# A decoder layer on one NeuronCore: 14 of 16 gate tiles by seven block products in a pass of their own, and the heads' filling laid out anew

## The chip, the core and the metric

The kernel is one program on one of the eight cores of a Trainium2 chip. The metric is the device time of one execution in microseconds (us). Five engines work at the same time, each through its own queue in its own order: PE (TensorE, matrix products and transposes into PSUM banks), DVE (VectorE), ACT (ScalarE), POOL (GpSimd) and SP (which here issues the DMAs). They wait for each other by semaphores.

## What is computed

A decoder layer on x (1024 tokens by 1024 channels, float32), cut here to what matters:

```python
x = x + 0.5 * swiglu(rms_norm(x, ffn1_norm), ...)          # 1024 -> 2816 -> 1024
h = rms_norm(x, mix_norm)
fq, fk, fv, f_logit, sq, sk, sv, g_fox, g_sb = split_columns(h @ w_in)
y_fox = forgetting_attention(rms_norm(fq), rms_norm(fk), fv, log_sigmoid(f_logit + bias))  # 8 heads of 64
y_sb  = stick_breaking_attention(sq, sk, sv)                                                # 8 heads of 64
merged = sigmoid(g_fox) * (y_fox @ w_branch_fox) + sigmoid(g_sb) * (y_sb @ w_branch_sb)
x = x + merged @ w_out
x = x + 0.5 * swiglu(rms_norm(x, ffn2_norm), ...)
x = x + sigmoid(rms_norm(x, ple_norm) @ w_ple_gate) * (p @ w_ple_proj)
```

The gates g_fox and g_sb are 2048 columns of h @ w_in, here 16 tiles of 128 channels by 1024 tokens. Forgetting attention is a causal softmax with a decay per key; stick-breaking attention weighs key s by a sigmoid times the product of (1 - sigmoid) over the keys between s and the query, a running product from right to left.

## The kernel before, in words

**Precision.** Every float32 operand of a product is split into a rounded high part (ACT copies) and a low part (the difference, by DVE or, for weights, by POOL: `wlow`, line 139). A product is three products: high·high, high·low, low·high. One gate tile is two halves of 512 tokens; one half is 3 x 8 matmuls of 128x512 (`feat_steps`, line 708).

**Seven block products.** The two feed-forward blocks don't multiply by the plain rule. `ffn` (line 380) cuts each pair of tiles into blocks and forms 7 products of 3 x 4 matmuls for what takes 8 by the plain rule (Winograd's form of Strassen's scheme; line 473 of the gate and up products, line 368 of the down product). The sums of blocks of h that it needs are made by the `combo_` functions: `a` turns a 128-token slice of the normalised h by transposes (line 228), the others make the sums and split them. The first block pair is partly taken by `plain` (line 428), plain products that run while the sums are made.

**The order.** Inside the feed-forward blocks all engines' orders are as written in the source. In attention, `pe(...)` ties PE's instructions to the written order, and `order("dve", ...)` and `order("act", ...)` tie some of those of DVE and ACT; the rest is placed by a scheduler when the program is built, and each engine then runs its list in order. A tile of a tag (`BUFS`, line 31) has a fixed number of buffers, and an instruction that writes one waits for the readers of what lay in it.

**Between the first feed-forward block and attention** (`mix_start`, line 1050). The last down products overlap with the norm of x; then come the value products of four heads (`v_units`, 8 units of one 128-token block each) and the query and key products of the first pair of forgetting heads (`fox_qk_units`, 8 units), each unit 24 matmuls of 256 or 264 columns (line 700). After unit 3 and unit 7 of a pair, the half of four units is normalised: ACT squares and copies (764, 765), DVE sums (766, 769), POOL takes the power -1/2 (770) and multiplies (772). Then come the sums of the forget gates (`forget_logs`, `forget_sums`, lines 909 and 910) and, plain, gate tiles 0 and 1 and the PLE projection (`p_units`, line 863).

**Stacks.** Per head, `fox_stack_units` turns the normalised queries and keys of one half of the tokens with four transposes (line 802, from the tile that line 772 wrote) and splits them into the tiles Q, KH and KL (787 to 790, two DMAs between partitions); `sb_stack_units` does so from products with 24 matmuls of 128x512 per half.

**The heads.** `attention` (line 1079) runs 16 heads, 8 forgetting (h 0 to 7) and 8 stick-breaking (h 8 to 15), each in four steps c = 0 to 3 of two 128-query blocks. A step does `scores` of its two blocks (PE lines 944 and 945) and then `apply` of the step before it: for each pair of key blocks, from the last to the first, four transposes of the weights (996), a high copy by ACT (998), a low part by DVE (999), and four value products (1018) that read both. In the stick-breaking heads ACT takes two sigmoids of the scores (952, 953), DVE does the running products (`scan`, 920) and POOL multiplies (967, 971). The scans of a step's first block are issued in `scores`; those of the second block (`later`) are issued inside `apply`, one after each low part.

**Filling.** `take` puts other matmuls between: 22 times per head (7, 4, 5 and 6 times in steps 0 to 3) it takes the next 1/22 of that head's entry of `fill`, a list of units written out by hand: value units, query and key units, the next head's stacks, and the plain gate tiles (`g_units`, line 821), tiles 2 to 15 in heads 2 to 15.

**After the heads** come the branch products, in which `gated` (line 1229) loads a gate half, takes its sigmoid (gates of the forgetting branch) and multiplies; the output product; and the second feed-forward block, entered through `second_entry` (line 1389), whose norm, transposes and sums run between the last output products and the first gate products.

Of the kernel before, what the change touches and what calls it, by code (L numbers as in the profile page):

```python
# [31 lines left out]
        "Q": 2, "KH": 2, "KL": 2, "Y": 2, "PT": 3}  # L32
# [4 lines left out]
def tile_hybrid_decoder_layer(  # L37
# [223 lines left out]
    def halves(N):  # L261
        return [(n["hi"], n["lo"]) for n in N]
# [117 lines left out]
    def ffn(N, wg, wu, wd, next_gain, resid, hid, tags, entry, tail):  # L380

        wsrc = [kp(w[0]) for w in (wg, wu)]
        wdown = wd[0].rearrange("(j k p) n -> k p j n", k=2, p=P)
        LA = 4
        nm_ = 2 * NF  # L390
# [4 lines left out]
        seqn += [(n, 1), (n - 1, 4), (n, 2), (n, 6), (n, 5), (n, 7), (n - 1, 3), (n, 3), (n, 4)]  # L395
# [9 lines left out]
        def load(n):  # L405
            f0 = n // 2 * 256
            W[n] = {"r": [slot(t, [P, 4, 256]) for t in tags["raw"].get(n, (("WH", "WH"), ("KH", "KL"))[n % 2])]}
            for kh in range(2):
                nc.sync.dma_start(W[n]["r"][kh][:], wsrc[n % 2][:, 4 * kh:4 * kh + 4, f0:f0 + 256])
# [23 lines left out]
        def silu(f_, half):  # L433
            if 0 not in E:
                E[0] = [slot(t, [P, 2, 512]) for t in ("GF", "RN")]
            nc.scalar.activation(E[0][f_][:, half, :], bank_of.pop("plain")[:], AF.Silu)
# [11 lines left out]
        def prep(n, m):  # L448
# [9 lines left out]
            if m == 3 and n + 2 < nm_:  # L458
                load(n + 2)
# [19 lines left out]

        def right(t, b, k):  # L480
            if isinstance(t, list):
                return t[2 * b + k // 2][:, k % 2, :]
            return t[:, b, k, :]

        def evict(n, m, ps):
# [8 lines left out]
            elif m == 7:  # L494
                nc.scalar.copy(e2[:, 1, :], ps[:])
                nc.vector.tensor_add(e2[:, 1, :], e2[:, 1, :], bank_of[n, "d"][:])
# [27 lines left out]
        C = {"w": {}, "t1": {}}  # L524

        def combo_a(q):

            h = N[1]["h"][q]
            cs = slice(q * P, (q + 1) * P)
            if q == 0:  # L530
                B[1], B[2] = N[0]["B"]
                B[3] = [slot("T", [P, 2, 512], F32R) for _ in range(4)]
                B["12"] = slot("X", [P, 2, 4, 512], F32R)
            w = C["w"][q] = slot(tags["w"][q], [P, 2, 4, P])
            v12, v22 = (turn(h, b, bank(cyc("t", ("pf", "av", "pf", "sc", "pt", "av", "pt", "sc")))) for b in range(2))
            nc.scalar.copy(w[:, 0], v12)
            nc.scalar.copy(w[:, 1], v22)
            split(B["12"][:, 0, :, cs], B["12"][:, 1, :, cs], w[:, 0], nc.scalar, nc.vector)
            for i in range(2):
                split(B[3][i][:, :, cs], B[3][2 + i][:, :, cs], w[:, 1, 2 * i:2 * i + 2], nc.scalar, nc.vector)  # L540

        def combo_t(q):

            cs = slice(q * P, (q + 1) * P)
            if q == 0:
                B[5] = slot("H", [P, 2, 4, 512], F32R)
            if q % 2 == 0:
                C["t1"][q // 2] = slot(("RN", "GF")[q // 2], [P, 2, 4, P])
            w, t1 = C["w"][q], C["t1"][q // 2][:, q % 2]
            nc.vector.tensor_sub(t1, w[:, 0], f(B[1][:, 0, :, cs]))  # L550
            nc.vector.tensor_sub(t1, t1, f(B[1][:, 1, :, cs]))
            nc.scalar.copy(B[5][:, 0, :, cs], t1)

        def combo_l(q):

            cs = slice(q * P, (q + 1) * P)
            nc.vector.tensor_sub(B[5][:, 1, :, cs], C["t1"][q // 2][:, q % 2], f(B[5][:, 0, :, cs]))

        def combo_u(q):

            w, t1 = C["w"][q], C["t1"][q // 2][:, q % 2]
            nc.vector.tensor_sub(w[:, 0], w[:, 1], w[:, 0])
            nc.vector.tensor_sub(w[:, 1], w[:, 1], t1)

        def combo_s(q, m):

            cs = slice(q * P, (q + 1) * P)
            if q == 0:
                B[m] = slot("H" if m == 6 else "X", [P, 2, 4, 512], F32R)
            split(B[m][:, 0, :, cs], B[m][:, 1, :, cs], C["w"][q][:, 7 - m], nc.scalar, nc.vector)  # L570

        def combo_d(q):

            cs = slice(q * P, (q + 1) * P)
            w = C["w"][q]
            nc.vector.tensor_sub(w[:, 0], f(B[2][:, 0, :, cs]), w[:, 1])
            nc.vector.tensor_add(w[:, 0], w[:, 0], f(B[2][:, 1, :, cs]))

        def combo_e(q):
            cs = slice(q * P, (q + 1) * P)  # L580
            if q == 0:
                B[4] = slot("X", [P, 2, 4, 512], F32R)
            split(B[4][:, 0, :, cs], B[4][:, 1, :, cs], C["w"][q][:, 0], nc.scalar, nc.vector)

        down = make_down(wdown, hid, [(0, 4), (4, 7), (7, 11)], 0.5, ("Y", "PT"))
        nxt = []

        def last_norms(i, t):
            if i == 4:
                norm_stat(nxt[0], t, ("PT", "PT", "KH", "KL")[t])  # L590
            elif i == 5:
                norm_mul(nxt[0], t)
            elif i == 6:
                if t == 3:
                    norm_post(nxt[0], 2, ps1)
                norm_stat(nxt[1], t, ("GF", "RN", "KH", "KL")[t])
                if t:
                    if t < 3:
                        norm_mul(nxt[1], t - 1)
                    norm_post(nxt[0], (None, 0, 1, 3)[t], ps1)  # L600
                for call in tail.get((i, t), ()):
                    call(nxt)

        manual[0] = True
        with tc.manual_schedule():
            entry(dict(a=combo_a, t=combo_t, l=combo_l, u=combo_u, s=combo_s, load=load, prep=prep, sums=sums, last_sum=last_sum, plain=plain, silu=silu, product=product, evict=evict))
            for s, (n, m) in enumerate(seqn):
                evict(n, m, product(n, m))
                if s == 0:
                    sums(2, nc.vector)  # L610
                    for q in range(4):
                        combo_s(q, 7)
                elif s == 2:
                    last_sum(1, nc.vector)
                    last_sum(2, nc.vector)
                if 1 < s < 6:
                    combo_d(s - 2)
                if 2 < s < 7:
                    combo_e(s - 3)
                if s + LA < len(seqn):  # L620
                    prep(*seqn[s + LA])
# [22 lines left out]
            for s, (c, i) in enumerate(steps):  # L644
# [18 lines left out]
                if final:  # L663
                    if i == 3:
                        nxt.append(norm_begin(X[0], next_gain))
                        nxt.append(norm_begin(X[1], next_gain, nxt[0]))
                    for call in tail.get(i, ()):
                        call(X)
                for t in range(4):
                    matmuls(t)  # L670
                    evict_down(t)
                    if final:
                        last_norms(i, t)
            norm_mul(nxt[1], 2)
            norm_mul(nxt[1], 3)
            tail["end"](X, nxt)
        manual[0] = False
        return X, nxt
# [621 lines left out]
    def products(F, rest=()):  # L1300

        F["load"](2)
        for i in range(2):
            F["plain"](1, 0, (i,))
            for q in rest[i:i + 1]:
                F["a"](q)
# [242 lines left out]
```

## Time and profile before

| | |
|---|---|
| median of 3 runs | 2273.2 us (2272.91 to 2273.32) |
| the profiled execution's own time | 2274.11 us |
| its span, first to last instruction | 2272.4 us |
| PE busy | 2248.2 us of the span (99%) |
| DVE, ACT, POOL busy | 1462.3, 977.4, 828.8 us |
| first forgetting head starts | 755.7 us from the span's start |
| first stick-breaking head starts | 1049.7 us |
| last value product of the last head | 1393.3 us |

Times in the views count from the span's start. A view of groups gives the line, engine and operation, what is written from what, the shape, the count, then the busy time and the mean duration of one (ns), then the idle time of the engine before them and what ended it. A timeline row is start, duration, engine, line, operation, and in brackets the engine's idle time before it. A matmul row is longer than the distance to the next matmul, since matmuls are pipelined; what a matmul costs is the distance between starts.

### The profile page before, as it was taken

What the parts mean: (1) busy time and instruction counts of PE and PEld (TensorE: products, weight loads), DVE (VectorE), ACT (ScalarE), POOL (GpSimd) and SP (SyncE); (2) the same over time, 40 slices, a digit from 0 to 9 for tenths busy, and PEclk for the clock granted to TensorE, in tenths of its full rate; (3) what the DMA queues carried; (4) which work ended last, traced back from release to release, by engine and by line L of the source; (5) the groups of instructions that cost most, each with busy time, mean ns of one, the idle gap of its engine ahead of it and who ended that gap; (6) DMA issues with size and microseconds to landing.
All of it is one profiled execution on the core that took longest, in us unless ns stands there. A gap on an engine that the chain in (4) does not pass through costs nothing. (4 is left out here: it accounts for less than half of the span.)

```text
span 2272.4 us, 30639 instructions
## 1 busy us (share of the span) xinstructions
PE 2248.2 (99%) x11462; PEld 1911.9 (84%) x11462; DVE 1462.3 (64%) x2199; ACT 977.4 (43%) x1741; POOL 828.8 (36%) x762
## 2 busy tenths in 40 slices
PE   8999999999999999999999999999999999999999
PEld 6888888888899999988988888888888888888888
DVE  8845555688863466666667676889655555778753
ACT  6333333333353555555555564246333333434431
POOL 2344444300033456554645644410544444200121
PEclk9999999999999999999999999999999999999999
DMA  4232323484333322132224245822423232756132
GB/s 139 99 120 85 124 84 125 152 302 171 103 122 121 103 80 75 48 89 70 52 56 116 61 144 176 299 109 65 139 84 125 84 125 80 263 194 218 60 103 84
DMA packets 187655, 275.49 MB, mean 121 GB/s; under 512 B 27113, under 2 KB 109417, under 8 KB 187506
## 3 DMA queue, kind: packets, MB, share of 16 engines
q1 hardware_dynamic: 187504, 273.53, 35.9%
q8 instruction: 90, 1.47, 0.3%
q14 instruction: 59, 0.48, 0.1%
q10 hardware_dynamic: 2, 0.00, 0.0%
HBM read 189.83 MB, written 75.27 MB: 117 GB/s over the span
## 5 line engine op out<-in xcount | busy, mean ns | idle before, releaser
L368 PE MATMUL ps<-H,H 128*128 128x512 f32 x2184 | 497.7, 389 | 1.2 <-DVE X L376 1.2
L368 PEld LDWEIGHTS ps<-H,H 128*128 128x128 f32 x2184 | 409.4, 188 | 86.7 <-issue 2.0
L473 PE MATMUL ps<-H,WL 128*128 128x512 f32 x1008 | 239.3, 389 | 0.8 <-ACT WL L105 0.8
L473 PEld LDWEIGHTS ps<-H,WL 128*128 128x128 f32 x1008 | 189.1, 188 | 40.4 <-ACT WL L105 1.2
L708 PE MATMUL ps<-H,WH 128*128 128x512 f32 x768 | 210.3, 401 | 1.1 <-DVE PT L831 1.1
L708 PEld LDWEIGHTS ps<-H,WH 128*128 128x128 f32 x768 | 136.4, 188 | 24.1 <-DVE PT L831 1.5
L139 POOL TENSOR_TENSOR WL<-RAW,WH 128x512 fp32r<-128x512 f32 (+1 forms) x108 | 127.4, 1200 | 77.5 <-ACT WH L129 71.9
L139 POOL TENSOR_TENSOR WL<-Y,WH 128x512 fp32r<-128x512 f32 (+1 forms) x10 | 14.4, 1466 | 382.6 <-ACT WH L129 382.6
L999 DVE TENSOR_TENSOR PT<-ps,PT 128x512 fp32r<-128x512 f32 (+1 forms) x160 | 101.1, 633 | 76.1 <-ACT PT L998 75.1
L473 PE MATMUL ps<-H,Q 128*128 128x512 f32 x600 | 143.1, 389 | 0.0
L376 DVE SCALAR_TENSOR_TENSOR X<-ps,X 128x512 f32<-128x512 f32 x168 | 109.0, 685 | 50.9 <-PE ps L368 50.9
L700 PE MATMUL ps<-WH,H 128*128 128x256 f32 (+1 forms) x896 | 132.0, 287 | 1.9 <-DVE X L106 1.0
L473 PEld LDWEIGHTS ps<-H,Q 128*128 128x128 f32 x600 | 112.6, 188 | 23.4
L998 ACT CAST PT<-ps 128x512 fp32r<-128x512 f32 (+1 forms) x160 | 87.3, 548 | 95.8 <-PE ps L996 92.3
L473 PE MATMUL ps<-X,WL 128*128 128x512 f32 x504 | 121.1, 389 | 0.0
L700 PEld LDWEIGHTS ps<-WH,H 128*128 128x128 f32 x896 | 116.9, 190 | 3.7 <-DVE X L106 1.4
L1018 PE MATMUL ps<-PT,X 128*128 128x256 f32 (+1 forms) x640 | 106.2, 283 | 6.1 <-DVE PT L999 6.0
L473 PEld LDWEIGHTS ps<-X,WL 128*128 128x128 f32 x504 | 94.6, 188 | 19.6
L1018 PEld LDWEIGHTS ps<-PT,X 128*128 128x128 f32 x640 | 94.5, 190 | 19.1 <-DVE PT L999 9.7
L708 PE MATMUL ps<-H,WL 128*128 128x512 f32 x384 | 108.3, 398 | 0.0
L957 POOL TENSOR_TENSOR T<-T,l 128x128 f32<-128x128 f32 (+3 forms) x64 | 73.3, 1150 | 88.5 <-DVE l L956 86.1
L269 POOL TENSOR_TENSOR PT<-GF,RN 128x512 f32<-128x512 f32 x20 | 33.1, 1655 | 186.0 <-DVE GF L516 101.8
(400 smaller groups left out, 4735.3 us busy)
## 6 DMA issues: line engine op xcount, KB each, us to landing
hidden<-PT SPq DMA_DIRECT2D x40, 512.0 KB, 3.1
WH<-in_ffn_w_gate_dram SPq DMA_DIRECT2D x38, 512.0 KB, 5.3
Q<-hidden SPq DMA_DIRECT2D x24, 512.0 KB, 6.1
hidden<-RN SPq DMA_DIRECT2D x22, 512.0 KB, 2.7
RAW<-in_w_in_dram SPq DMA_DIRECT2D x22, 512.0 KB, 4.3
KH<-in_ffn_w_up_dram SPq DMA_DIRECT2D x20, 512.0 KB, 6.2
KL<-in_ffn_w_up_dram SPq DMA_DIRECT2D x20, 512.0 KB, 6.8
T<-in_ffn_w_down_dram SPq DMA_DIRECT2D x20, 512.0 KB, 4.3
```

Source lines behind the costliest of these rows:

```text
L139: ins = eng_lo.tensor_sub(lo[part], raw[part], f(hi[part]))
L269: eng.tensor_add(s12[:, 0, :], g1[:, 1, :], g2[:, 1, :])
L368: pe(nc.tensor.matmul(groups[g][t][:], act[:, a, k, t * P:(t + 1) * P], wt[:, b, k, :], start=(fresh and n == 0), stop=(i in (6, 1, 4) and ...
L376: nc.vector.scalar_tensor_tensor(xs, groups[g][t][:], scale, xs, ALU.mult, ALU.add)
L473: pe(nc.tensor.matmul(ps[:], hl[:, a, k, :], rhs(m, b, k), start=(first and i == 0), stop=(final and i == 11), skip_group_check=True))
L700: pe(nc.tensor.matmul(ps[:, :n], hT[t // 4][a][:, k, (t % 4) * P:(t % 4 + 1) * P], w[k // 4][b][:, k % 4, :n], start=(i == 0), stop=(i == ...
L708: pe(nc.tensor.matmul(ps[:], w[a][:, k, :], hT[half][b][:, k, :], start=(i == 0), stop=(i == 23)))
L957: nc.gpsimd.tensor_mul(T[:, :n], T[:, :n], l[:].broadcast_to([P, n]))
L998: high = nc.scalar.copy(pt[:, 0, :width], ps[:, :width])
L999: low = nc.vector.tensor_sub(pt[:, 1, :width], ps[:, :width], f(pt[:, 0, :width]))
L1018: pe(nc.tensor.matmul(o, lh, r, start=(kpair == c and i == 0), stop=(kpair == 0 and i == 3)))
```

## The change

`ffn`'s block products become `make_up`, used by both feed-forward blocks and by a new pass over the gates; `up_begin`, `up_step` and `up_first` are what `second_entry` did, and are now called by the gates' pass as well. The main parts:

```diff
-        "Q": 2, "KH": 2, "KL": 2, "Y": 2, "PT": 3}
+        "Q": 2, "KH": 2, "KL": 2, "Y": 2, "PT": 3, "Z": 2}
...
+    NG = 7
     def mix_start():
...
+        def gate_out(n, i, e):
+            nc.sync.dma_start(gd[2 * n + i].rearrange("p (h n) -> p h n", h=2), e[:])
...
+        F = make_up(N, lambda n: kp(win)[:, :, GFOX + n * 256:GFOX + n * 256 + 256], NG, tags_g, AF.Sigmoid, gate_out, load_qk)
...
-        def end(X, N):
-            hT.extend(halves(N))
-            store_x(X, 1)
...
-            side = posts(N[1], (24, 64, 104, 144), lambda: bank("pt"))
-            side[48] = [lambda: mx["qk"].update(w=[wsplit(raws["qk"][kh], 4, 256, tags[kh]) for kh in range(2)])]
-            weave(seq(*[g for _, g in mx["u1"][:4] + mx["u2"][:4]]), side)
+        def end():
+            up_first(N, F)
+            seqn = up_order(NG)
+            L = len(seqn)
+            for s, (n, m) in enumerate(seqn):
+                evict(n, m, F.product(n, m))
+                F.begin(s)
+                if s + 4 < L:
+                    F.prep(*seqn[s + 4])
...
+            for _, g in mx["u1"]:
+                run(g)
```

In attention, the part ahead of the heads and the filling:

```diff
-        run_all(u1[4:])
         sums = forget_logs(wk)
-        run_all(p0[:1] + u2[4:])
+        run_all(p0[:1] + u2)
         forget_sums(sums)
         f0 = fst(0, any_bank)
-        run_all(g0[:1] + f0[:1] + p0[1:3] + g0[1:] + f0[1:] + p0[3:] + g1[:1] + p1 + g1[1:])
+        run_all(f0[:1] + p0[1:3] + f0[1:] + p0[3:] + p1)
-        fill.append(mix(fst(1), fox_qk_units(fox_pairs[1], qk[1])))
-        fill.append(uv[:4] + mix(fst(2), uv[4:]))
-        fill.append(mix(fst(3), g + uq[:4]))
-        fill.append(uq[4:] + mix(fst(4), g_units(3)))
-        fill.append(mix(fst(5), fox_qk_units(fox_pairs[3], qk[3])))
-        fill.append(uv[:4] + mix(u, uv[4:]))
...
-        fill.append(u + g9[1:] + g10)
-        u, g11, g12 = sst(13), g_units(11), g_units(12)
-        fill.append(u + g11 + g12[:1])
...
+        fill = [mix(fst(1), qk1[:6]),
+                qk1[6:] + fst(2) + vx[:4],
+                fst(3) + vx[4:] + uq2[:2],
+                uq2[2:] + fst(4),
+                fst(5) + uq3[:5],
+                uq3[5:] + fst(6) + vy[:2],
+                fst(7) + vy[2:7],
+                vy[7:] + s8,
+                s9 + vz[:2],
+                vz[2:6] + s10,
+                vz[6:] + s11,
+                s12 + g14[:1],
+                g14[1:] + s13,
+                s14 + g15[:1],
+                g15[1:] + s15,
+                fox_branch[:7]]
```

Here `fst(h)` are the two stack units of forgetting head h, `sst(h)` or `s8` to `s15` those of stick-breaking heads, `qk1`, `uq2`, `uq3` (`uq`) the query and key units of the second to fourth pair, `uv`, `vx`, `vy`, `vz` value units, `g14` a gate tile's two halves. All gates are now written out after their sigmoid, and `gated` loses it:

```diff
     def gated(dst, ps, gate, m, half):
         nc.sync.dma_start(dst, gd[gate * KD + m, :, half * 512:half * 512 + 512])
-        order("act", nc.scalar.activation(dst, dst, AF.Sigmoid))
         nc.vector.tensor_mul(dst, dst, ps[:])
```

The gates' pass keeps h as the operands of its sums, so that later products read h through small functions in place of two tiles; two new buffers (Z) hold part of one sum, for which the scratch space of dynamic DMAs goes from 8192 to 4096 bytes.

530 lines of the change are left out of this document (294 added, 236 removed).

## The prediction

> **What bounds the kernel now.** First the page: one engine is busy from end to end.
>
> ```profile
> PE 2248.2 (99%) x11462; PEld 1911.9 (84%) x11462; DVE 1462.3 (64%) x2199; ACT 977.4 (43%) x1741; POOL 828.8 (36%) x762
> ```
>
> Busy PE need not be PE at its pace, so next the chain of work that ended last, and PE's waits.
>
> ```profile
> 1566.89 394.40 PE ps L473 x1740
> ```
>
> ```profile
> PE ps L1018 <- DVE PT L999: 6.0, 10, 1.7
> ```
>
> 1740 block-product matmuls in 394.40 us are 0.2267 us each, without a hole. The longest sum of waits inside the kernel is 6.0 us: value products waiting for DVE's low parts. So the time is PE's matmul count plus few holes, and a change pays by fewer matmuls and costs by new holes. Three stretches matter: the entry to the new pass, the forgetting heads (755.7 to 1049.7 us) and the stick-breaking heads (1049.7 to 1393.3 us).
>
> **Matmuls removed.** 14 plain gate tiles are 14 x 2 x 24 = 672 matmuls. The pass has 4 plain half products of 24 and 7 products of 12 for six of its seven pairs: 96 + 504 = 600. Transposes stay (64 moved). 72 x 0.2267 = **-16.3 us**. It can't be more, and it is less only if the pass has holes. Its evictions, splits and DMAs are of the second feed-forward block's kinds, whose 1740 matmuls above run without one.
>
> **Entry.** It is the second feed-forward block's entry once more. There PE waits twice:
>
> ```profile
> 1535.28 1.09 PE L228 MATMUL ps<-identf,PT 128*128 128x128 f32 x8 [0.99 <-DVE H L106]
> 1536.77 1.09 PE L228 MATMUL ps<-identf,PT 128*128 128x128 f32 x8 [0.40 <-ACT Q L536]
> ```
>
> **+1.4 us** (0 to 3). The pass's stores and weight loads go to SP's queue, from which PE waits for nothing inside the kernel; the smaller DMA scratch and one more table load of ACT (bounds 0 and 2 us) I take at nothing, covered by the matmuls of the products in flight.
>
> **Stacks behind their own normalisation.** After a pair's last unit ACT, DVE and POOL must normalise the second half before its transposes can start. PE, timeline:
>
> ```profile
> 707.16 0.64 PE L700 MATMUL ps<-Y,H 128*128 128x256 f32 x4
> ...
> 711.10 3.92 PE L708 MATMUL ps<-H,WH 128*128 128x512 f32 x16
> ```
>
> POOL, the same half:
>
> ```profile
> 712.16 1.91 POOL L772 TENSOR_TENSOR RN<-RN,qkss 128x1024 f32<-128x1024 f32 x1
> ```
>
> From the last unit's end (707.64) to the multiply's end (714.07) are 6.4 us. Before, gate tile 0 stands behind 711.10 on PE, and the stacks' transposes follow; the changed list has those of half 0 (0.4 us) and at once those of half 1: wait 714.07 - 711.10 - 0.4 = **+2.6 us** (0 to 6). Everything behind on PE waits too; the projection's operands are split long before.
>
> Inside the heads it is worse. In the second pair, PE and POOL:
>
> ```profile
> 788.62 1.12 PE L700 MATMUL ps<-WL,H 128*128 128x256 f32 x8
> ```
>
> ```profile
> 789.46 5.04 POOL L139 TENSOR_TENSOR WL<-RAW,WH 128x512 fp32r<-128x512 f32 x4 [5.39 <-ACT WH L129]
> 794.45 2.92 POOL L770 TENSOR_TENSOR qkss<-qkss,mhalf 128x16 f32<-128x16 f32 x1
> 797.44 1.91 POOL L772 TENSOR_TENSOR RN<-RN,qkss 128x1024 f32<-128x1024 f32 x1
> ```
>
> The unit ends at 789.6, the multiply at 799.35: 9.8 us, because four weight splits stand ahead of the power. In the third pair two stand ahead:
>
> ```profile
> 880.10 1.12 PE L700 MATMUL ps<-WL,H 128*128 128x256 f32 x8
> ```
>
> ```profile
> 887.19 1.91 POOL L772 TENSOR_TENSOR RN<-RN,qkss 128x1024 f32<-128x1024 f32 x1
> ```
>
> 881.05 to 889.10, 8.05 us. Before, value units or a gate half lie between a pair's last unit and the stacks' second half. The changed fill sets `fst(2)`, `fst(4)`, `fst(6)` right behind the last units of three pairs. In the changed PE list only a few transposes, scores and four value products lie between: at the starts above some 1.3, 0.9 and 0.8 us. With the middle chain, 3 x 8.05 - 3.0 = **+21.2 us**; bounds 3 x 6.4 - 3.0 = 16.2 and 3 x 9.8 - 3.0 = 26.4 (POOL's changed list has four splits ahead in all three). Queued behind on PE are that head's scores and values, so all engines lose this time.
>
> Also, both stack halves now follow each other, and the unit behind needs the first one's PSUM bank: four more waits of the length of this one's, partly hidden, **+1.5 us** (0 to 6).
>
> ```profile
> 892.62 0.73 PE L708 MATMUL ps<-H,WH 128*128 128x512 f32 x2 [0.68 <-DVE PT L831]
> ```
>
> **Stick-breaking heads with less to fill.** Six of them (8, 10 to 14) lose about two gate halves each (120 matmuls of filling to 72), 10.9 us, or 0.495 us at each of 22 places; heads 9 and 15 half of it. The four steps of head 11 as windows (length, then busy PE, PEld, DVE, ACT, POOL):
>
> ```profile
> 1175.80:1188.80 13.00, 13.00 (x77) 11.21 (x76) 5.62 (x10) 4.77 (x11) 2.12 (x5) 1.00 0.17 46
> 1188.80:1195.62 6.82, 6.82 (x36) 5.66 (x34) 3.89 (x8) 4.67 (x9) 4.08 (x5) 1.00 0.00 0
> 1195.62:1204.84 9.22, 9.22 (x52) 7.97 (x51) 8.40 (x11) 5.72 (x13) 7.77 (x9) 1.00 0.44 115
> 1204.84:1216.75 11.91, 11.91 (x66) 10.03 (x64) 9.49 (x11) 7.76 (x15) 8.45 (x8) 1.00 0.29 68
> ```
>
> PE's work would shrink by 7, 4, 5 and 6 places to 9.5, 4.8, 6.7 and 8.9 us. Steps 0 and 1 have DVE room for it; in steps 2 and 3 DVE is busy 8.40 and 9.49 us, more than PE would need. DVE in step 3:
>
> ```profile
> 1203.57 0.66 DVE L999 TENSOR_TENSOR PT<-ps,PT 128x512 fp32r<-128x512 f32 x1
> ...
> 1207.01 0.60 DVE L920 TENSOR_TENSOR_SCAN RN<-GF,mask_sb 128x128 f32<-128x128 f32 x1 [1.01 <-ACT GF L952]
> 1207.65 2.07 DVE L920 TENSOR_TENSOR_SCAN RN<-GF,RN 128x383 f32<-128x383 f32 x2
> 1210.46 0.56 DVE L999 TENSOR_TENSOR PT<-ps,PT 128x384 fp32r<-128x384 f32 x1 [0.74 <-ACT PT L998]
> 1210.94 1.13 DVE L920 TENSOR_TENSOR_SCAN RN<-GF,mask_sb 128x128 f32<-128x128 f32 x1
> ...
> 1215.57 0.66 DVE L999 TENSOR_TENSOR PT<-ps,PT 128x512 fp32r<-128x512 f32 x1
> ```
>
> The last low part of step 2 ends at 1204.23, that of step 3 at 1216.23: a cycle of 12.0 us, in which DVE idles only 1.0 us (for sigmoids of scores that PE may issue only after that low part) and 0.7 us (for ACT's copy). I shorten it by most of the second: 11.3 us against PE's 8.9, so 2.4 us of waiting. Step 2's cycle, here and in head 8, where POOL does less beside it:
>
> ```profile
> 1194.67 0.56 DVE L999 TENSOR_TENSOR PT<-ps,PT 128x384 fp32r<-128x384 f32 x1
> ```
>
> ```profile
> 1068.62 0.56 DVE L999 TENSOR_TENSOR PT<-ps,PT 128x384 fp32r<-128x384 f32 x1
> ...
> 1073.94 0.69 DVE L831 COPY PT<-ps 128x512 f32<-128x512 f32 x1
> ...
> 1076.40 0.67 DVE L999 TENSOR_TENSOR PT<-ps,PT 128x512 fp32r<-128x512 f32 x1
> ```
>
> 1195.23 to 1204.23 is 9.0 us; 1069.18 to 1077.07, less a gate's copy that goes, is 7.2 us. Against PE's 6.7 that is 0.5 to 2.3 us of waiting, together 2.9 to 4.7. I take 3.5, towards head 8, since fewer weight splits on POOL share the stretch. Six heads x 3.5 + two x 1.75 = 24.5, less the holes that are there already:
>
> ```profile
> 755.70:1049.70 294.00, 289.79 (x2074) 271.31 (x2073) 180.08 (x563) 159.91 (x346) 166.72 (x169) 1.00 0.25 70
> 1049.70:1393.30 343.60, 337.64 (x1908) 291.15 (x1907) 235.82 (x333) 195.06 (x407) 192.98 (x214) 1.00 0.33 96
> ```
>
> 343.6 - 337.6 = 6.0. So **+18.5 us** (0 to 28). In the forgetting heads DVE is busy 180 of 294 us, and of the 250 or so that less filling leaves still only 0.7: there I add nothing for the pace.
>
> **Sum.** -16.3 + 1.4 + 2.6 + 21.2 + 1.5 + 18.5 = +28.9. The profiled execution took 2274.1 us, 0.9 above the median: 2303.0, by the median **2302 us**.
>
> **Rivals.** (a) *Only one of the two large costs comes.* If the stick-breaking heads follow PE, 2302 - 18.5 = 2283.5; if the chains of the three pairs are hidden, 2302 - 21.2 = 2281. For the first: the same 128-column scan took 0.60 and 1.13 us above, so its length hangs on something beside it that may thin out. Against the second: POOL's own 2.9 + 1.9 us stand in every chain.
>
> (b) *POOL lightened*, the one that ends on the other side. 12 gate tiles less in the heads are 24 weight splits less on POOL. If these lengthen scans and chains, the stick-breaking heads follow PE (0 instead of 18.5), the chains fall to 6.4 us (16.2 instead of 21.2) and no bank wait comes: 2302 - 18.5 - 5.0 - 1.5 = 2277, within 0.2% of before. It decides only where DVE's work of steps 2 and 3, 17.9 us now, fits into PE's 15.6; faster still only where a chain is hidden as well, against all three rows.
>
> (c) *A slow PE after the waits.* In the first microseconds, after 5 us without matmuls, transposes went slower than soon after:
>
> ```profile
> 11.00 1.72 PE L228 MATMUL ps<-identf,PT 128*128 128x128 f32 x8 [0.35 <-DVE PT L223]
> ...
> 14.68 1.06 PE L228 MATMUL ps<-identf,PT 128*128 128x128 f32 x8 [0.20 <-DVE PT L223]
> ```
>
> Eight took 1.72, then 1.06 us. If each of the three waits of some 7 us slows PE to 1.06 / 1.72 of its pace for 4 to 7 us, it loses 1.5 to 2.7 us, 5 to 8 in all: 2307 to 2310. For it: the start; against it: it was a start, and no later row has such a wait. The Trainium skill ("TensorE: Matmul & The Clock Gate", Part 1) has a rule that speaks against this change: after an idle window of about 3.4 us the gate passes half the clock until PE has been busy about as long. By it the loss is an estimated 1.7 us a wait, 5 in all, so 2307; the start agrees with it, and nothing inside this trace idles long enough to show it.
>
> **Chances.** Forecast 0.42, (c) 0.23, (a) 0.25, (b) 0.10, of which 0.04 faster. The range takes in (c) and the upper bounds in part and nearly all of (a): 2281 to 2322. About 0.2% is what a measurement can tell from no change: faster 0.04, same 0.06, slower 0.90.
>
> **What would show it.** Right: PE waits for RN at three stack transposes, 6 us or more each, with four weight splits ahead of the power on POOL; value products waiting for low parts sum to over 20 us; the gates' pass runs at 0.2267 us a matmul. Wrong: stick-breaking heads of 30 to 31 us, or the power not queued behind splits.

## The result and the profile after

The changed kernel took 2352.1 us (median; 2351.4 to 2352.6 in three executions) against 2273.3 for the one before (2272.9 to 2273.6): 1.0346 times as long, 95% interval 1.0326 to 1.0366, 79 us more. One further execution ran at a mean granted clock of 0.84 and took 2546 us; it is left out, so the rows below are of one more execution of the same kernel, 2355.9 us. The forecast was 2302 us, 2281 to 2322: the sign was right, the size was not.

The page of the changed kernel; the last row gives the granted clock in 40 slices:

```profile
span 2354.2 us, 30693 instructions
...
PE 2265.6 (96%) x11390; PEld 1921.2 (82%) x11390; DVE 1528.5 (65%) x2306; ACT 1011.2 (43%) x1818; POOL 812.0 (34%) x747
...
PEclk9999999999999999988999999999999999999999
```

PE has 72 matmuls fewer, as forecast, and is no longer busy throughout. In stages (length, busy time and count of PE, PEld, DVE, ACT and POOL, then the granted clock, the DMA engines' busy share and their GB/s): a piece of the new pass, the forgetting heads, the stick-breaking heads.

```profile
660.00:840.00 180.00, 180.00 (x966) 156.15 (x965) 99.34 (x187) 83.91 (x156) 41.52 (x31) 1.00 0.33 108
874.50:1173.30 298.80, 253.25 (x1835) 240.34 (x1834) 170.36 (x550) 154.07 (x342) 154.24 (x159) 0.92 0.19 52
1173.30:1475.00 301.70, 274.82 (x1572) 235.77 (x1571) 236.29 (x332) 174.33 (x375) 178.82 (x200) 0.97 0.30 85
```

The pass has no hole. The forgetting heads lost 239 matmuls and got longer, 298.8 us against 294.0. The stick-breaking heads lost 76 us of matmuls and got 42 us shorter (301.7 against 343.6). In both the clock is below 1. PE's waits in the forgetting heads (what PE wrote, its line, what it waited for: us in total, times, longest), then in the stick-breaking heads:

```profile
PE ps L901 <- POOL RN L871: 27.3, 3, 9.7
PE ps L799 <- DVE KL L889: 8.6, 3, 3.0
PE ps L1114 <- ACT PT L1094: 3.6, 6, 1.0
PE ps L1114 <- DVE PT L1095: 1.9, 4, 1.2
PE ps L901 <- DVE KL L889: 1.6, 1, 1.6
```

```profile
PE ps L1114 <- DVE PT L1095: 25.8, 24, 2.0
```

The three waits for RN are the three stacks of the forecast. POOL before the first of them, and PE behind it, have the queue that it described: four splits (4.97 us), the power, the multiply.

```profile
912.34 4.97 POOL L139 TENSOR_TENSOR WL<-RAW,WH 128x512 fp32r<-128x512 f32 x4 [0.84 <-ACT WH L129]
917.27 2.91 POOL L869 TENSOR_TENSOR qkss<-qkss,mhalf 128x16 f32<-128x16 f32 x1
920.26 1.90 POOL L871 TENSOR_TENSOR RN<-RN,qkss 128x1024 f32<-128x1024 f32 x1
```

```profile
922.21 1.11 PE L901 MATMUL ps<-identf,RN 128*128 128x128 f32 x4 [8.26 <-POOL RN L871]
```

New is the clock. Windows around this wait, and around a wait of 2.8 us that ends at 949.0:

```profile
912.80:916.20 3.40, 1.15 (x9) 0.88 (x8) 2.67 (x8) 3.31 (x8) 3.40 (x4) 1.00 0.06 9
916.20:926.40 10.20, 4.19 (x18) 4.00 (x19) 3.09 (x9) 1.40 (x3) 7.10 (x6) 0.50 0.53 137
926.40:929.80 3.40, 3.40 (x29) 3.40 (x29) 1.93 (x6) 1.92 (x5) 1.50 (x3) 1.00 0.18 42
946.90:950.30 3.40, 1.29 (x11) 1.32 (x12) 2.68 (x8) 2.37 (x5) 1.01 (x2) 1.00 0.26 60
950.30:953.70 3.40, 3.40 (x18) 3.40 (x18) 1.61 (x3) 1.06 (x2) 0.00 (x0) 0.50 0.43 99
953.70:957.10 3.40, 3.40 (x31) 3.40 (x31) 1.25 (x3) 1.34 (x3) 0.48 (x2) 1.00 0.00 0
```

With the clock at 0.50 PE does 18 matmuls in 3.4 us, right after that 31. The kernel before has no such stretch ahead of its last half microsecond; this one has 13 between 851 and 1466 us, 71 us in all.

**Where the 79 us are.** Matmuls have usual distances between their starts (0.2267 us for 512 columns, 0.12 for 256, 0.109 for 128). What a start comes later is a wait, or, while the clock is 0.50, up to one more such distance, slow clock. Summed over stages, in us, before and after (the split between waits and slow clock is good to about 1 us):

| stage | matmuls | waits | slow clock |
|---|---|---|---|
| ahead of the heads | (all matmuls -16.3) | 0.5 to 4.4 | 0 to 1.6 |
| forgetting heads | 286.4 to 232.0 | 7.6 to 55.0 | 0 to 11.9 |
| stick-breaking heads | 330.1 to 253.9 | 13.6 to 39.2 | 0 to 8.7 |

-16.3 + 3.9 + 47.4 + 25.6 + 22.2 = +82.8; the two spans differ by 81.8, since the first matmul came 1.0 us earlier. (This execution is 3.8 us above the median.)

### The profile page after: what moved, and what is told of

It reads as the page before. It is cut to its first block, busy times and chain, and to the rows that moved or that the text cites. A ratio compares the mean times of both kernels' runs of the same rounds, so it can differ in the third digit from the quotient of the medians.

```text
span 2544.2 us, 30693 instructions
## 1 busy us (share of the span) xinstructions
PE 2470.8 (97%) x11390; PEld 1977.8 (78%) x11390; DVE 1501.3 (59%) x2306; ACT 1013.5 (40%) x1818; POOL 807.4 (32%) x747
## 4 chain that ended last, share of the span: by engine, by line
PE 89%; DVE 5%; issue 2%; POOL 2%; ACT 2%; DMA 0%; SPq 0%; DVEq 0%; ACTq 0%; POOLq 0%
PE ps L556 40%; PE ps L454 22%; PE ps L799 6%; PE ps L1552 4%; PE ps L1357 3%; DVE RN L1016 3%; PE ps L506 3%; PE ps L807 3%; PE ps L1114 3%; PE ps L1092 2%; PE ps L228 1%; PE ps L1041 1%; PE ps L1040 1%; PE ps L959 1%; DVE PT L1095 1%
## 5 line engine op out<-in xcount | busy, mean ns | idle before, releaser
L454 PE MATMUL ps<-H,H 128*128 128x512 f32 x2184 | 550.0, 417 | 0.0
L556 PE MATMUL ps<-H,WL 128*128 128x512 f32 x1128 | 295.3, 417 | 0.0
L556 PEld LDWEIGHTS ps<-H,WL 128*128 128x128 f32 x1128 | 216.4, 192 | 66.6
L556 PE MATMUL ps<-X,WL 128*128 128x512 f32 x588 | 155.7, 417 | 0.0
L799 PE MATMUL ps<-WH,H 128*128 128x256 f32 x768 | 133.7, 310 | 8.4 <-DVE KL L889 7.9
L139 POOL TENSOR_TENSOR WL<-RAW,WH 128x512 fp32r<-128x512 f32 (+1 forms) x80 | 94.2, 1203 | 82.1 <-ACT WH L129 48.8
L556 PE MATMUL ps<-H,PT 128*128 128x512 f32 x456 | 120.0, 417 | 0.0
L556 PEld LDWEIGHTS ps<-H,PT 128*128 128x128 f32 x456 | 87.4, 192 | 26.8
L1016 DVE TENSOR_TENSOR_SCAN RN<-GF,RN 128x127 f32<-128x127 f32 (+2 forms) x96 | 102.0, 1063 | 2.7
L807 PE MATMUL ps<-H,WH 128*128 128x512 f32 x320 | 101.1, 431 | 0.0
## 6 DMA issues: line engine op xcount, KB each, us to landing
X<-in_x_dram SPq DMA_DIRECT2D x16, 512.0 KB, 10.1
```

The source lines that it names most:

```text
L139: ins = eng_lo.tensor_sub(lo[part], raw[part], f(hi[part]))
L454: pe(nc.tensor.matmul(groups[g][t][:], act[:, a, k, t * P:(t + 1) * P], wt[:, b, k, :], start=(fresh and n == 0), stop=(i in (6, 1, 4) and ...
L556: pe(nc.tensor.matmul(ps[:], hl[:, a, k, :], rhs(m, b, k), start=(first and i == 0), stop=(final and i == 11), skip_group_check=True))
L799: pe(nc.tensor.matmul(ps[:, :n], hT[t // 4](a, k)[:, (t % 4) * P:(t % 4 + 1) * P], w[k // 4][b][:, k % 4, :n], start=(i == 0), stop=(i == ...
L807: pe(nc.tensor.matmul(ps[:], w[a][:, k, :], hT[half](b, k), start=(i == 0), stop=(i == 23)))
L1016: order("dve", nc.vector.tensor_tensor_scan(*args))
```

## The experiments

Times are medians; the kernel before took 2272.9 to 2273.8 beside each group of runs. Heads are counted from 0.

**The changed kernel again.**

> The changed kernel unchanged, for a profile at its usual pace (the profile at hand has a granted clock of 0.84 from end to end, three other executions 0.985). Theory A, a slow clock behind waits: the granted clock is 1.00 outside the heads and clearly lower in a few stretches inside them, each right behind a PE wait of 7 us or more; matmuls there are further apart than 0.2267 us, and these stretches lose some 30 to 50 us in all. Theory B, more waiting than forecast: the clock is 1.00 wherever PE works, and PE's holes in the heads add up to about 95 us instead of 50.

2355.9 us; its rows are those above. Both theories hold in part: outside the heads the clock is 1.00 but for one stretch of 3.4 us, and the slow clock costs 22 us in all, less than 30 to 50; the waits in the heads, holes in PE's work, are 94 us instead of 21, as theory B had it. The slow stretches do not stand behind long waits only.

**Units between a pair's last unit and its stacks.**

```diff
-                qk1[6:] + fst(2) + vx[:4],
-                fst(3) + vx[4:] + uq2[:2],
-                uq2[2:] + fst(4),
+                qk1[6:] + f2[:1] + vx[:4] + f2[1:],
+                fst(3) + vx[4:] + uq2[:4],
+                uq2[4:] + f4[:1] + [(5.2, gap(5.2))] + f4[1:],
...
-                uq3[5:] + fst(6) + vy[:2],
+                uq3[5:] + f6[:1] + vy[:2] + f6[1:],
```

`gap` issues nothing and only counts as 5.2 us of filling, so that attention's own work comes between.

> The changed kernel with value units (two pairs) or attention's own work (the third) between a pair's last unit and the second half of its stacks, so that the three long PE waits go; work and count of matmuls are the same. Forecast's size: the three waits cost 21 us and about 4 of bank waits, so 2327 us. Theory A (slow clock behind each of these waits): they cost twice that or more, so 2290 to 2310 us, with a granted clock back at 1.00. Theory B (the time is in the pace of the stick-breaking heads): 2325 to 2335 us, and the heads from the ninth on take as long as in the changed kernel.

2331.2 us (1.0257, 1.0240 to 1.0274): 21 us less. By the same sums the forgetting heads have 16.3 us less waiting and 5.1 less slow clock; the long waits went, but smaller ones came. Stick-breaking heads kept their 39 us. The three waits are real, and a quarter of the loss.

**All stack halves apart.**

```diff
-                fst(3) + vx[4:] + uq2[:4],
+                vx[4:5] + f3[:1] + vx[5:6] + f3[1:] + vx[6:] + uq2[:4],
...
-                fst(5) + uq3[:5],
+                f5[:1] + [(2.6, gap(2.6))] + f5[1:] + uq3[:5],
...
-                fst(7) + vy[2:7],
+                vy[2:3] + f7[:1] + vy[3:4] + f7[1:] + vy[4:7],
```

> As the run with units between, and the two stack halves of heads 3, 5 and 7 kept apart too, by value units or by attention's own work. Theory stacks: the waits of a following unit for the first half's bank (about 2 us each) and for the second half go, with the slow clock behind them: 12 to 16 us less than 2331, so 2315 to 2319 us. Theory thin filling: what is gained there comes back as other waits in the same heads, 2325 to 2333 us.

2326.2 us (1.0233, 1.0216 to 1.0250), 5 us less, the better end of thin filling. The waits for RN are gone, and the forgetting heads still have 36 us of holes, spread over other things:

```profile
PE ps L1114 <- DVE PT L1095: 7.4, 9, 1.7
PE ps L1092 <- POOL T L1053: 7.2, 5, 2.4
PE ps L1114 <- ACT PT L1094: 4.7, 5, 2.2
```

**PE kept busy in the long waits.**

```diff
             ps = new_bank()
+            if half and new_bank is fill_bank and hh == 0:
+                for k in range(32):
+                    pe(nc.tensor.matmul(ps[:], hT[0](0, k % 8)[:, 0:P], hT[0](0, k % 8), start=True, stop=True))
             for q in range(4):
```

> The changed kernel with 32 matmuls of 512 columns more ahead of the transposes of the second stack half of heads 2, 4 and 6, whose products nobody reads: they take 7.3 us of PE in waits of 8.4 to 9.9 us, so the waits end at the same time, but PE works through them. Theory A (slow clock behind waits is a cost of its own): no half clock behind these three waits, 4 to 6 us less than the changed kernel, 2346 to 2348 us against 2352. If the slow clock costs nothing: 2352, the same, or a little more where a matmul delays the transposes.

2346.8 us (1.0324, 1.0309 to 1.0340), 5.3 below the changed kernel; the two intervals overlap, so the rows decide. Heads 1, 3 and 5 with the extra matmuls:

```profile
903.00:943.30 40.30, 38.84 (x287) 36.67 (x286) 22.32 (x70) 20.69 (x45) 23.59 (x23) 1.00 0.20 53
977.80:1020.40 42.60, 39.86 (x287) 36.84 (x286) 21.66 (x71) 20.62 (x49) 27.05 (x24) 1.00 0.18 45
1058.10:1100.40 42.30, 37.78 (x262) 34.07 (x262) 21.76 (x70) 20.35 (x46) 25.39 (x26) 1.00 0.21 51
```

The clock is 1.00 in all three (0.88 to 0.90 in the changed kernel), and with 96 more matmuls the three heads are 3.1 us shorter (125.2 against 128.3). Slow clock behind a wait is a cost of its own.

**No gates in the heads, no pass.** In the list of `fill` of the kernel before, every `g_units` after tile 1 is taken out, and the branch products read the gate tile's number modulo 2.

> The kernel before with gate tiles 2 to 15 left out (they are not computed; the branch products read tiles 0 and 1 in their place): less filling in the heads, and no new pass. 672 matmuls less are 152.3 us, so 2121 us if the heads follow PE. Theory thin filling (both kinds of heads have a length of their own of some 30 to 35 us, set by the other engines and by waits along the way from transposes to value products): heads 2, 3, 6 and 7 and all eight stick-breaking heads open holes, 60 to 90 us in all, 2180 to 2210 us, although the fillings' order is that of before. Theory order (the loss comes from how the changed filling is laid out, with stacks in a row): few holes, 2121 to 2150 us.

2204.2 us (0.9697, 0.9682 to 0.9711). 152.3 us of matmuls less give 69: thin filling, with the old order and without the pass. Forgetting heads, then stick-breaking heads:

```profile
754.30:1026.00 271.70, 246.40 (x1835) 232.23 (x1834) 171.72 (x551) 153.00 (x340) 154.27 (x159) 0.96 0.21 57
1026.00:1319.30 293.30, 255.62 (x1476) 214.80 (x1475) 235.88 (x332) 176.91 (x384) 168.70 (x196) 0.97 0.28 79
```

**Eight tiles by blocks instead of 14.** As the run with all stacks apart, and `NG = 4`, with tiles 8 to 15 as filling of heads 8 to 14 (`g_units`, about three halves a head, as before the change).

> The pass takes 8 gate tiles in place of 14 (4 pairs), and the stick-breaking heads get 8 plain tiles of filling back; forgetting heads as in the run before this one. 36 matmuls fewer than in the kernel before (-8.2 us) instead of 72. Theory thin filling: the stick-breaking heads lose their holes nearly wholly (39 us of waits there against 14 in the kernel before; 15 to 20 here) and the forgetting heads keep theirs, 2285 to 2300 us. If the stick-breaking heads' pace does not hang on their filling: 2320 us and more.

2309.2 us (1.0159, 1.0144 to 1.0174), 17 less than with 14 tiles and above the forecast: the stick-breaking heads came out as theory filling had it, the forgetting heads cost more than I had put. The stick-breaking heads are back at a clock of 1.00, with 18.3 us of waits:

```profile
816.10:1092.30 276.20, 251.08 (x1835) 236.37 (x1834) 170.63 (x550) 154.56 (x343) 154.31 (x159) 0.96 0.21 56
1092.30:1429.80 337.50, 327.97 (x1860) 281.73 (x1859) 235.69 (x332) 186.96 (x394) 193.10 (x212) 1.00 0.32 95
```

Six tiles (288 matmuls, 65.3 us) put back made these heads 40.5 us longer (337.5 against 297.0), 62% of it.

**The pass and the old filling together.** The changed kernel with the whole `fill` of the kernel before.

> The changed kernel with the filling of the kernel before: the pass computes 14 gate tiles, and the heads compute tiles 2 to 15 once more by the plain rule (the second results overwrite the first). Theory filling (the pass itself runs without holes, and the heads' loss comes from nothing but the filling): 2273 + 600 matmuls of the pass (136.0) - 96 of tiles 0 and 1 (21.8) + 3.9 of waits ahead of the heads = 2391 us, within 3, heads as long as in the kernel before and the granted clock 1.00. Rival, the pass or what it holds (two new buffers, smaller DMA scratch, more table loads) disturbs the heads or itself: 2398 us or more.

2399.2 us (1.0555, 1.0541 to 1.0570), 8 more than by filling alone; the rival's number, though little of it is in the pass:

```profile
660.00:840.00 180.00, 180.00 (x967) 156.12 (x966) 99.63 (x187) 84.01 (x156) 41.41 (x31) 1.00 0.33 108
874.60:1175.50 300.90, 292.18 (x2075) 271.35 (x2074) 174.56 (x552) 190.14 (x377) 166.85 (x169) 1.00 0.25 69
1175.50:1519.00 343.50, 338.19 (x1908) 291.18 (x1907) 235.18 (x330) 188.04 (x395) 192.67 (x214) 1.00 0.33 96
```

The pass runs without a hole, the stick-breaking heads take their old time, the forgetting heads 6.9 us more than before, in many waits of about 1 us, and 1.6 us of slow clock stand ahead of them. So of the changed kernel's 47 us there, up to 7 come with the pass and not with the filling; which of its parts does it was not tried.

**Less work for DVE.** The left scan of `scores` is left out:

```diff
-                    scan(R[:, 0:cut][:, ::-1], G[:, 1:cut + 1][:, ::-1], G[:, 1:cut + 1][:, ::-1], R[:, cut:cut + 1], ALU.mult, ALU.bypass)
-                    nc.gpsimd.tensor_mul(T[:, :cut], T[:, :cut], R[:, :cut])
+                    nc.gpsimd.tensor_mul(T[:, :cut], T[:, :cut], G[:, :cut])
```

> The changed kernel without the left part of the running products of the stick-breaking heads (the scan over the left half of the keys is not computed; POOL multiplies by the plain factors there instead, so POOL, PE and ACT do what they did). Theory DVE (steps 2 and 3 of these heads last as long as DVE works, and value products wait for low parts that are queued behind scans): PE's waits in these heads fall from 39 us to 15 or less, 20 to 35 us less than 2352 with the slow clock that goes along. Theory latency (the way from transposes over ACT's copy and DVE's low part to the values is too long for the thin filling, whatever DVE has queued): less than 8 us.

2334.8 us (1.0269, 1.0252 to 1.0286), 17 less, between the two. Waits in the stick-breaking heads fell from 39.2 to 26.0 us, slow clock from 8.7 to 0. Steps 2 and 3 together fell from 20.6 to 18.6 us a head (heads 8 to 14), with DVE at 13.8 instead of 19.1. DVE's scans set part of these steps; something else comes soon behind.

**Filling moved to the late steps.** On the run with all stacks apart:

```diff
-                state[0] += total / 22
+                state[0] += total / 22 * (1 if fox else (0.43, 0.43, 1.46, 1.66)[at[0]])
```

> As the run with all stacks apart, but in the stick-breaking heads the filling is not spread evenly over the 22 places: places in steps 0 and 1 take 0.43 of the even share, those in steps 2 and 3 take 1.46 and 1.66 times it. Theory DVE: steps 2 and 3 stay at DVE's 8.4 and 11.9 us however much PE has in them up to that, and steps 0 and 1, which follow PE, get shorter by 4.7 us of filling moved away, less what their own chains then show: 1.5 to 3.5 us in each of eight heads, 2298 to 2314 us. Theory latency: waits go where the filling was taken from, 2320 to 2330 us.

2326.3 us (1.0234, 1.0218 to 1.0249): nothing gained, as theory latency had it. **To the early steps**, with (1.45, 1.45, 0.55, 0.55):

> The opposite of the run with filling in the late steps: places in steps 0 and 1 of the stick-breaking heads take 1.45 times the even share, those in steps 2 and 3 take 0.55 of it (the stacks' halves, which come first in each list, so fall into steps 0 and 1). Over heads 8 to 14, steps 0 and 1 together take 14.7 us a head and steps 2 and 3 take 20.6 in the run with all stacks apart, where DVE is busy 19.7 of the 20.6. Theory DVE full: 3.7 us of PE's work leave steps 2 and 3, but these get shorter only by DVE's stack splits that leave with them, 1 to 1.5 us, while steps 0 and 1 get longer by what they take in, 3 to 4 us: 2338 to 2350 us. Theory PE's work alone counts: steps 2 and 3 get shorter by what the others get longer, 2322 to 2330 us.

2360.2 us (1.0384, 1.0367 to 1.0401), 34 more and outside both ranges: over heads 8 to 14, steps 2 and 3 stayed at 20.6 us a head although DVE's work in them fell from 19.1 to 18.0 us, and steps 0 and 1 went from 14.7 to 19.0. **Half as far to the late steps**, with (0.7, 0.7, 1.25, 1.34):

> As the run with filling in the late steps, but half as far: 0.7 of the even share in steps 0 and 1, 1.25 and 1.34 times it in steps 2 and 3, so 2.4 us of PE's work a head move in place of 4.7. Steps 2 and 3 took 20.6 us a head with PE busy 17.3 in four kernels whatever their filling, and 23.4 with PE busy 22.0 in the one that had 4.7 us more. If DVE sets 20.6 until PE's work comes near it, they stay at 20.6 to 21.2 here (PE 19.7), steps 0 and 1 fall from 14.7 to about 13, and the kernel takes 2312 to 2320 us against 2326. If nothing is to be had by moving, 2324 to 2328.

2318.7 us (1.0199, 1.0182 to 1.0216), 8 less, inside the first range. Head 12 of these kernels, steps 0 and 1, then 2 and 3 (length, PE, PEld, DVE): the one before, the changed one, filling early, filling late, half as far.

```profile
1216.75:1236.57 19.82, 19.82 (x110) 16.86 (x108) 9.89 (x18) 9.55 (x21) 8.64 (x12) 1.00 0.47 138
1236.57:1258.55 21.98, 21.49 (x114) 17.98 (x114) 17.41 (x21) 12.27 (x26) 15.38 (x15) 1.00 0.36 97
```

```profile
1316.58:1330.81 14.23, 14.12 (x85) 12.19 (x84) 8.32 (x13) 7.87 (x17) 6.17 (x9) 1.00 0.29 98
1330.81:1350.88 20.07, 16.91 (x91) 14.06 (x91) 19.59 (x26) 13.28 (x28) 15.10 (x17) 0.97 0.34 111
```

```profile
1311.93:1329.75 17.82, 17.82 (x101) 15.30 (x100) 7.85 (x15) 9.15 (x19) 6.77 (x11) 1.00 0.27 90
1329.75:1349.13 19.38, 15.21 (x74) 11.64 (x74) 16.77 (x23) 12.04 (x26) 12.55 (x14) 0.91 0.29 96
```

```profile
1292.83:1303.96 11.13, 10.34 (x64) 8.48 (x63) 6.68 (x14) 7.30 (x16) 3.81 (x8) 1.00 0.35 95
1303.96:1325.64 21.68, 20.97 (x111) 17.47 (x111) 18.55 (x23) 13.38 (x28) 16.18 (x17) 1.00 0.35 125
```

```profile
1289.84:1301.95 12.11, 11.96 (x75) 10.25 (x73) 6.72 (x13) 7.86 (x17) 3.73 (x8) 1.00 0.30 96
1301.95:1322.94 20.99, 19.02 (x102) 15.51 (x101) 19.12 (x24) 12.74 (x27) 16.11 (x17) 1.00 0.35 121
```

In head 12, steps 2 and 3 take 19.4 to 20.1 us with PE busy 15.2 or 16.9, and 21.0 with PE busy 19.0; steps 0 and 1 follow PE. Over heads 8 to 14 the mean of steps 2 and 3 is 21.9 us before, 20.6 in the changed kernel, with all stacks apart and with filling early, 22.0 half as far and 23.4 with filling late. So the late steps have a length of their own, not far above DVE's work in them (18.0 to 19.1 us). Half as far, 2.5 us more of PE's work cost them 1.4 us, and steps 0 and 1 fell by 2.2, from 14.7 to 12.5. Moving 4.7 us filled the late steps up to PE's work (22.0 of 23.4 us) and opened waits in the early ones (11.8 us, PE busy 10.6). What sets the 20.6 us besides DVE is not shown.

**Splits on DVE.** `mix_nat` passes `nc.vector` as the engine of the low parts.

> The changed kernel with the low parts of the weights of the query, key and value units in the heads made by DVE in place of POOL, so that no weight split stands ahead of the power and the multiply of a pair's normalisation. Forecast's mechanism (POOL's queue): the three long waits fall from 8.4, 9.9 and 9.4 us to some 6 each, some waits for POOL's weights of the attention heads go too, 8 to 14 us less than 2352. Rival: the splits only change places, DVE's low parts of the weights delay the value products' operands, within 4 us of 2352.

2346.6 us (1.0323, 1.0307 to 1.0338), 5.6 less, between the two. The waits for RN fell to

```profile
PE ps L901 <- POOL RN L871: 22.0, 3, 8.1
```

instead of 27.3. The end of DVE's sums and the start of the power tell how much of such a wait is POOL's queue; the first row is of the changed kernel, the second of this run:

```profile
914.15 0.74 DVE L868 TENSOR_SCALAR qkss<-qkss 128x16 f32<-128x16 f32 x1
```

```profile
913.88 3.63 POOL L869 TENSOR_TENSOR qkss<-qkss,mhalf 128x16 f32<-128x16 f32 x1 [3.51 <-DVE qkss L868]
```

In the changed kernel the sums were done at 914.89 and the power began at 917.27, 2.4 us later; at the other two stacks it was 3.6 and 2.4 us, 8.3 of the 27.3 in all. Without that queue (in this run the power began 0.1, 0.1 and 1.1 us behind the sums) only 5.3 us were gained: the splits now stand on DVE, some of them ahead of the sums. The power and the multiply themselves, 2.9 + 1.9 us, are 14.4 us of the three waits. **Those three together** (stacks apart, late steps, splits on DVE):

> All stacks apart, filling in the late steps of the stick-breaking heads, and those splits on DVE. If the gains are of separate waits they add: 2326 less 12 to 28 less about 5 of the last (its long waits are gone already), 2293 to 2309 us. If they share what they save: not below the better one of the two by itself. For the kernel before (2273) to be reached, the forgetting heads, too, would have to be at their old distance from PE's work, which none of the three does.

2326.2 us (1.0232, 1.0217 to 1.0247): no better than either of the first two by itself.

**Value products two behind.** On the run with all stacks apart, and on the kernel before:

```diff
-        turn_and_scan(c)
-        for kpair in range(c - 1, -1, -1):
+        lag = 1 if step["fox"] or c == 0 else 2
+        for kpair in range(c, c - lag, -1):
+            turn_and_scan(kpair)
+        for kpair in range(c - lag, -1, -1):
             turn_and_scan(kpair)
-            values(kpair + 1)
+            values(kpair + lag)
...
-        values(0)
+        for kpair in range(lag - 1, -1, -1):
+            values(kpair)
```

> As the run with all stacks apart; in the stick-breaking heads the value products of a pair of key blocks are issued behind the transposes of the second next pair in place of the next one, so that ACT's copy and DVE's low part have a whole further round of PE's work as cover; all work is the same. Theory way too long (thin filling leaves too little PE work between transposes and value products; DVE has some time to spare): PE's waits in these heads fall from 39 us to 20 or less, 2300 to 2312 us. Theory DVE full (low parts and scans fill DVE in steps 2 and 3, so that products wait wherever they stand): 2320 us and more.

2328.3 us (1.0246, 1.0232 to 1.0260; not told apart from 2326.2): the waits stay, and steps 2 and 3 at 20.6 us a head. Products wait wherever they stand. A full DVE would do that, but with filling early DVE had only 18.0 us of work in the same 20.6 us, so that a full DVE is the whole reason is not shown.

```profile
PE ps L1114 <- DVE PT L1095: 23.8, 21, 2.2
```

> The kernel before with the same edit of the order of value products in the stick-breaking heads. Its waits there are 13.6 us in all: if the way is too long, up to 6 us of them go, 2267 to 2271 us, less than both kernels; if DVE is full, 2273 us as it was, or a little more where the tile of weights is held longer.

2281.6 us (1.0037, 1.0023 to 1.0050), slower, mostly by one wait for ACT's copy in head 12, and a slow clock behind it:

```profile
PE ps L1018 <- ACT PT L998: 4.5, 1, 4.5
```

No version here that computes all gates beats the kernel before; the best of the changed ones is the one with eight tiles.

## Why the prediction was wrong

| term of the sum, us | forecast | measured |
|---|---|---|
| matmuls | -16.3 | -16.3 |
| entry and stacks ahead of the heads | +4.0 | +3.9 |
| three pairs' stacks | +21.2 | +27.3 |
| bank waits behind stacks | +1.5 | +10.2 |
| rest of the forgetting heads | 0 | +9.9 |
| stick-breaking heads | +18.5 | +25.6 |
| slow clock | 0 (rival: 5 to 8) | +22.2 |

The sum came out 53.9 us short (28.9 against 82.8). Of these the slow clock is 22.2, the forgetting heads' other waits 18.6 (8.7 for banks, 9.9 for the rest), the stick-breaking heads 7.1, the three stacks 6.1.

**Right** were the matmuls, the pass that runs like the second feed-forward block, its entry, and the places: RN behind POOL's queue at three stacks, low parts of DVE in the late steps. All three signs named for "right" came (waits for RN of 8.3 to 9.8 us, over 20 us of waits for low parts, a pass without holes), but none of them tells of the terms that failed.

**Two steps failed. The first is "there I add nothing for the pace"** of the forgetting heads, and with it the way the price of filling was reckoned: from DVE's busy share of 180 in 294 us. No engine but PE is nearly full there, and still PE waits as soon as the filling is thin. With all stacks apart these heads had 36 us of waits instead of 7.6 and took 274.2 us: of 54.4 us of filling taken out, 20 came back. The kernel without gates in the heads, with its old order and without the pass, came out nearly the same there (271.7 us), so it is the thin filling and not its new order. What the filling covers, by the waits that the views name, are chains from one PE instruction over other engines to the next one that reads the result (transposes, ACT's copy, DVE's low part, values; POOL's multiply ahead of the transposes). No run shortened such a chain in the forgetting heads, so this reason is argued, not shown. The bank waits, too, are such a chain, a stack's copies before its bank is free: three of 2.8 to 3.0 us and one of 1.6, taken at 1.5 us in all as partly hidden. Up to 7 us of the waits in these heads come with the pass even under the old filling; by what is open. **The second is the slow clock at nothing**, told further down.

**The three stacks** were sized from the middle chain (8.05 us) although four splits stood ahead in all three. Reckoned the same way, from the last unit's end to the multiply's end, the chains took 9.6, 11.6 and 10.1 us (912.52 to 922.16, 1010.54 to 1022.16, 1081.01 to 1091.15); less the 3.0 of cover that is 28.4, near the 27.3 measured. So the reckoning held and the chain was mis-sized; the bound of 26.4 was the better value.

**The stick-breaking heads** had the right mechanism in part: 5.3 us less of DVE's work shortened steps 2 and 3, but by 2.0 us only. Steps 2 and 3 were put at 19.1 us together (3.5 us of waiting over PE's 15.6) and took 20.6. The new lists bring more of the stacks' splits of DVE into them, 1.7 us a head instead of 0.6.

**The slow clock was a rival**, priced rightly for the three long waits (4.9 us by the same sums, 5.3 in the run that kept PE busy), but left out of the sum and taken to need them. Ten more stretches stand behind shorter holes, some of them two of 1 to 1.5 us close together, and cost 17 us. Rival (a) fell, neither large cost stayed away; (b) fell: the stick-breaking heads did not follow PE, and none of the three chains got shorter.

**Where the gain went.** From the second pair on, a pair of gate tiles takes 96 plain matmuls (21.8 us) out of the heads and puts 84 (19.0 us) into the pass. It pays only if the heads get shorter by more than seven eighths of what they lose. With their filling spread evenly the stick-breaking heads gave back 55 to 62%; with filling early it was 18%, half as far to the late steps 69%, the most of all runs that compute everything. The forgetting heads gave back at best 41%, and without the pass both together 48% (72.6 of 152.3 us).

## What to carry to other kernels

Work that fills holes has no price of its own: before moving it away, find what a stage takes without it (take it out, and look at the length), and compare the share that comes back with the share that the new place costs. A low busy share of the other engines doesn't say that a stage will follow PE when it gets thinner; look at the chains over other engines from one PE instruction to the next that reads its result. Moving filling inside a stage helps only where the stage has a length of its own and only up to it.

## What the hardware showed that I had not expected

The granted clock of PE falls to 0.50 in stretches of 3.4, 6.8 or 10.2 us, in this kernel 13 times, and not only after long waits: a wait of 1.8 us that ended at 1196.28 sufficed, while one of 2.0 us that ended at 1418.42 had no such stretch behind it.

```profile
1196.28 1.01 PE L1114 MATMUL ps<-PT,X 128*128 128x256 f32 x3 [1.78 <-DVE PT L1095]
1418.42 0.50 PE L1114 MATMUL ps<-PT,X 128*128 128x128 f32 x2 [2.01 <-DVE PT L1095]
```

The trace shows a pattern. The 13 stretches begin whole multiples of 3.413 us apart, so they lie on one grid of windows, and whether one begins goes with PE's busy time in the window of that grid just ahead. The first hole lies nearly all in one window, the second is shared by two:

```profile
1192.70:1196.10 3.40, 1.66 (x12) 1.30 (x11) 3.36 (x4) 1.32 (x3) 3.40 (x5) 1.00 0.00 0
1196.10:1199.50 3.40, 3.22 (x12) 3.04 (x13) 3.22 (x5) 1.75 (x5) 3.19 (x3) 0.50 0.54 121
1414.50:1417.90 3.40, 1.91 (x12) 1.51 (x10) 3.33 (x5) 2.19 (x5) 0.88 (x1) 1.00 0.73 204
1417.90:1421.30 3.40, 1.75 (x10) 1.34 (x10) 3.36 (x5) 1.85 (x3) 2.44 (x4) 1.00 0.96 294
1421.30:1424.70 3.40, 1.84 (x10) 1.43 (x11) 3.40 (x4) 1.78 (x3) 2.24 (x2) 1.00 0.72 276
```

In this execution every window at full clock with PE busy for 1.7 us or less has a window at half clock behind it, no window with 1.9 us or more has one, and in between there is one of each. In the other runs' traces the border lies between 1.5 and 2.2 us, so busy time as the profile models it is not all of the rule. The Trainium skill ("TensorE: Matmul & The Clock Gate", Part 1) describes windows of about 3.4 us that run freely; the lengths of the stretches agree with it, while waits shorter than a window that had this effect go beyond its rule of an idle window. Repeated executions of the thinner kernels spread by 1 to 8 us where the kernel before spreads by under 1; where the grid lies against the heads differs from trace to trace and could explain it, but only one execution of each kernel is traced, so that it is not shown.
